# Block 0 of a hybrid encoder kernel: v and ca from unsplit fp32, low parts on the vector engine, and two changed load orders

## The chip, the cores and the metric

The kernel runs on one core of a Trainium2 chip. The core has a matmul engine (PE, with its weight loads shown as PEld), a vector engine (DVE), an engine for activation functions and copies (ACT), a general engine (POOL), a queue engine that issues most transfers (SP), and 16 DMA engines that all queues share. Each engine runs its own instructions in the order in which the compiler put them, and waits for the others by semaphores. The metric is the device time of one execution in microseconds, the median over several runs. "Granted clock" is the share of full speed at which the chip lets PE run.

## What is computed

One layer of an encoder trunk over 2048 tokens of width 1024, in float32. The parts that matter here:

```python
mod = silu(c) @ w_ada + b_ada                    # 1024 x 3072
shift, scale, gate = split(mod, 3)
h = rmsnorm(x, norm_g) * (1 + scale) + shift     # "adaLN"
u = h @ w_in + b_in                              # 1024 x 4364
mq, mk, mv, mo, mz, mi, mf, fq, fk, fv, fz, ff, ca, cg, cz = split(u)
ya = mlstm(silu(conv4(mq, mk)), mv, mi, mf, mo) * silu(mz)   # 4 heads of 128
yb = forgetting_attention(fq, fk, fv, ff) * silu(fz)         # 4 heads of 64, "fox"
yc = layernorm_silu(conv31(ca * sigmoid(cg))) * silu(cz)     # 256 channels
y = concat(ya, yb, yc) @ w_out
out = rmsnorm(x + gate * y, final_g)
```

## The kernel before, in words

**Blocks and units.** The tokens are worked in four blocks of 512 (b = 0 to 3). For each block `hprep` (L123) makes the normalised, modulated input h, transposed so that the 1024 features lie on the partitions as 8 tiles of 128 x 512. The columns of `w_in` are worked in units of 256 columns, in the order of the list `useq` (L200): v, ca, cg, then twice mv, mo, two of qk and mz, then fz, cz, f0 and f1. Units v, f0, f1 and fz are the attention's values, queries, keys and gate; ca, cg and cz are the convolution's; the m units are the mLSTM's. The last block has a slightly different order (v late). A unit with 128 weight columns as its left operand (`mm_cm`, L265) makes two groups of matmuls 128 x 512; one with tokens on its left (`mm_tm`, L277: v, mv, mo) makes four groups of 256 columns.

**Precision.** Products are made in the format fp32r, three for each pair of operands: the high part of a value is its copy in fp32r, the low part is what is left of it. So each of h and w is split in a high part (hh, wh) and a low part (hl, wl), and a group of 8 feature tiles has 24 matmuls: wh hh, wh hl and wl hh. A matmul of two plain fp32 operands exists too, in the mLSTM and in the sum for the gate, for example.

**Weights.** In block 0, `split_unit` (L161) loads each unit's two halves raw (512 KB each, tag "wr", two buffers), copies them to the high part on ACT (L177), subtracts on POOL for the low part (L178) and writes both parts to a scratch tensor `wd` in HBM from POOL's queue (L179, 1 MB for each half). In later blocks `reload_unit` (L184) loads the two parts back. The split tiles (tag "w") have four buffers, so two units. `prefetch` (L226) prepares the next unit; `load_unit` (L236) calls it when fewer than two are ready, then issues up to six pending steps of the 31-tap convolution on DVE (`backlog`, L433; 60 for each block), then a pending stage of the mLSTM, then a step of `wout_steps` (only in block 1: the output weights times the gate, split and stored).

**The start.** `ada_k` (L720) is called from `hprep(0)` between its steps. It loads the adaLN weights for shift and scale in four pieces of 2 MB (L714: two transfers of 1 MB each; three buffers, `WAB`), and, per piece, multiplies its eight 128 x 512 slices by silu(c): two on ACT (L737), six on DVE in two chains (L739), and adds the two (L741). Eight tiny matmuls (`pt_ada`, L746) sum over partitions, and three small DVE instructions make `shift` and `gs` for two feature tiles. Then ACT applies them to the transposed x (`hf`, L149), copies the high part (`hh`, L152), and POOL (six tiles) or DVE (two) subtracts (`hl`, L153). On SP's queue come in this order: the first adaLN piece, the four x tiles of 512 KB, raw v, the second piece, raw ca, the third and fourth pieces, small biases (`later`). The scaling of x by its norm is done by DVE (L139) in all blocks.

**The end.** After block 3's projections `prep_out` (L974) loads the split output weights, 1 MB for each of 8 feature tiles. The first (`EP` = 1) is issued ahead of f0's unit, two more ahead of f1's. The output projection's loads of y and x (`out_load`) are issued as it begins.

**Order.** The program lists its work in the order of the source; a scheduler orders each engine's instructions by a simulated timeline, with earlier ones first where both are ready. `tc.issue_after(i)` keeps what is issued in its block behind instruction i on the same engine. POOL cannot read PSUM, where matmuls land; DVE and ACT can.

Of the kernel before, what the change touches and what calls it, by code (L numbers as in the profile page):

```python
# [38 lines left out]
def tile_hybrid_trunk(  # L39
# [83 lines left out]
    def hprep(b, pre=None):  # L123
        xts = []
        if pre is not None:
            pre(-1)
        for tt in range(NTT):
            xt = xkpool.tile([P, D], F32, name=f"x{b}_{tt}", tag="x")
            with tc.issue_after(wload["mz0_1"]) if b == 1 else ExitStack():
                dma.dma_start(xt, x[0, b * TB + tt * P : b * TB + (tt + 1) * P, :])  # L130
            s2 = xpool.tile([P, 2], F32, name=f"s2{b}_{tt}", tag="s2", bufs=4)
            for n in range(2):
                sq = xpool.tile([P, TB], F32, name=f"sq{b}_{tt}{n}", tag="hf", bufs=HFB)
                s.activation(sq, xt[:, n * TB : (n + 1) * TB], AF.Square, accum_out=s2[:, n : n + 1])
# [3 lines left out]
            g.tensor_tensor(ss, ss, nhalf[:, 0:1], op=ALU.pow)  # L138
            v.tensor_scalar(xt, xt, ss, None, op0=ALU.mult)  # L139
            xts.append(xt)  # L140
        hi, lo = [], []
        for k in range(KT):
            if pre is not None:
                pre(k)
            pt = psx.tile([P, 512], F32, name=f"xT{b}_{k}", tag="x")
            for tt in range(NTT):
                pe.transpose(pt[:, tt * P : (tt + 1) * P], xts[tt][:, k * P : (k + 1) * P], ident)
            hf = xpool.tile([P, TB], F32, name=f"hf{b}_{k}", tag="hf", bufs=HFB)
            s.activation(hf, pt, AF.Identity, bias=shift[:, k : k + 1], scale=gs[:, k : k + 1])  # L149
            hh = hhpool.tile([P, TB], F32R, name=f"hh{b}_{k}", tag="hh")  # L150
            hl = hpool.tile([P, TB], F32R, name=f"hl{b}_{k}", tag="hl", bufs=HLB)
            s.copy(hh, hf)  # L152
            (g if b == 0 and k < HLV else v).tensor_tensor(hl, hf, hh.bitcast(F32), op=ALU.subtract)  # L153
            hi.append(hh)
            lo.append(hl)
        return hi, lo


    w_d, wload = {}, {}

    def split_unit(name, pieces, pool):  # L161

        width = sum(n for _, n in pieces)
        w_d[tuple(pieces)] = wd = scratch.tile([2, P, 8 * width], F32, name=f"wd_{name}")
        whs, wls = [], []
        for hf in range(2):
            wr = pool.tile([P, 4, 268], F32, name=f"wr_{name}_{hf}", tag="wr", bufs=2)[:, :, 0:width]
            o = 0
            for col, n in pieces:
                wload[name] = dma.dma_start(  # L170
                    wr[:, :, o : o + n],
                    dram(w_in, hf * 4 * P * DIN + col, [[DIN, P], [P * DIN, 4], [1, n]]),
                ).ins
                o += n
            flat, w4 = unit_tile(name, hf, width)
            wh, wl = w4[:, 0], w4[:, 1]
            s.copy(wh, wr)  # L177
            g.tensor_tensor(wl, wr, wh.bitcast(F32), op=ALU.subtract)  # L178
            g.dma_start(wd[hf], flat.bitcast(F32))  # L179
            whs.append(wh)  # L180
            wls.append(wl)
        return whs, wls

    def reload_unit(name, pieces):  # L184

        wd = w_d[tuple(pieces)]
        width = sum(n for _, n in pieces)
        whs, wls = [], []
        for hf in range(2):
            flat, w4 = unit_tile(name, hf, width)  # L190
            dma.dma_start(flat.bitcast(F32), wd[hf])
            whs.append(w4[:, 0])
            wls.append(w4[:, 1])
        return whs, wls
# [31 lines left out]
    def prefetch(pool=wraw):  # L226
        if upos[0] < len(useq):
            name, pieces = useq[upos[0]]
            uready.append((name, reload_unit(name, pieces) if tuple(pieces) in w_d else split_unit(name, pieces, pool)))
# [47 lines left out]
    def mm_tm(name, w, h, tt, width):  # L277
        ps = proj_psum(f"pt_{name}")
        cs = slice(tt * P, (tt + 1) * P)
        n = 0  # L280
        for k in range(KT):
# [125 lines left out]
    def units_conv(b, h):  # L407
        wa = load_unit(f"ca{b}")
        av = []
        for m in range(2):  # L410
# [5 lines left out]
            av.append(f)  # L416
        wg = load_unit(f"cg{b}")
# [266 lines left out]
    with tc.tile_pool(name="ada", bufs=4, side="right") as apool:  # L684
# [29 lines left out]
        def ada_load(jp):  # L714
            wt = apool.tile([P, KT, 2, 256], F32, name=f"wa{jp}", tag="wa", bufs=WAB)
            for i in range(2):
                dma.dma_start(wt[:, :, i, :], dram(w_ada, i * D + jp * 256, [[3 * D, P], [P * 3 * D, KT], [1, 256]]))
            wts.append(wt)

        def ada_k(j):  # L720
            if j < 0:
                ada_load(0)
                return
            if j == 0:
# [5 lines left out]
                for a in later:  # L730
                    dma.dma_start(*a)
            if j % 2:
                return
            wt = wts[j // 2]
            accs = [apool.tile([P, 2, 256], F32, name=f"wacc{j}{e}", tag=f"wacc{e}", bufs=1 + e) for e in range(2)]
            for k in range(2):
                s.activation(accs[k], wt[:, k], AF.Identity, scale=csil[:, k : k + 1])  # L737
            for k in range(2, KT):
                v.scalar_tensor_tensor(accs[k % 2], wt[:, k], csil[:, k : k + 1], accs[k % 2], op0=ALU.mult, op1=ALU.add)  # L739
# [10 lines left out]
            v.scalar_tensor_tensor(gs[:, j : j + 2], gs[:, j : j + 2], 1.0, cols[:, R_NG + j : R_NG + j + 2],  # L750
                                   op0=ALU.add, op1=ALU.mult)

        h = hprep(0, ada_k)

        pt = psx.tile([P, 512], F32, name="pt_cols2", tag="x")
        pe.transpose(pt[:, R_BQK:R_END], r3, ident[0 : R_END - R_BQK, 0 : R_END - R_BQK])
        pe.transpose(pt[:, 256:318], r2, ident[0:62, 0:62])
        v.tensor_copy(cols[:, R_BQK:R_END], pt[:, R_BQK:R_END])
        v.tensor_scalar(colsh, cols, 0.5, None, op0=ALU.mult)
        v.tensor_scalar(dww, pt[:, 256:318], 0.5, None, op0=ALU.mult)  # L760
        v.tensor_scalar(colse, cols[:, R_BFQ : R_BFQ + 2], 0.125, None, op0=ALU.mult)
# [257 lines left out]
    def outproj(qd):  # L1019
# [4 lines left out]
        if qd == 0:  # L1024
            for tt, n in ((0, 0), (0, 1), (1, 0)):
                if n == 0:
                    if tt:
                        out_load(qd, tt)
# [40 lines left out]
    for b in range(NB):  # L1069
        if b == 1:  # L1070
            side += wout_steps()
        if b < NB - 1:
# [64 lines left out]
    free_hh.append(1)  # L1137

# [37 lines left out]
EP = 1  # L1176
# [13 lines left out]
WAB = 3  # L1190
HLV = 6
# [29 lines left out]
```

## Time and profile before

| | us |
|---|---|
| median of 3 runs | 1361.3 |
| lowest, highest | 1360.88, 1370.79 |
| the profiled execution | 1369.51 |
| its span (first to last instruction) | 1367.7 |
| PE busy in the span | 1278.7 |
| DVE, ACT, POOL busy | 957.8, 561.9, 391.2 |
| mean granted clock | 0.979 |

The rows shown below are from the profiled execution. A group's row has: line, engine, operation, result and operands by the program's names, shape, count; then busy time in us and the mean of one in ns; then the idle time of the engine just before these instructions and which instruction ended it. A row of the timeline has start and length in us. A row of the list of waits has who waited for whom, us in total, times, the longest. In the table by stage each engine's busy us stand with the count of its instructions in brackets, then the granted clock, the DMA engines' busy share and the GB/s that they moved.

### The profile page before, as it was taken

The numbers are of one execution on the slowest core, as the hardware profiler recorded it, in microseconds if no ns is written. First come the engines' busy times: TensorE is split into PE (matmuls) and PEld (weight loads), VectorE is DVE, ScalarE is ACT, GpSimd is POOL, SyncE is SP. The second block draws the span as 40 slices with busy tenths as digits, with TensorE's granted clock in tenths as the row PEclk, the third lists the DMA queues.
The fourth block names the chain that finished last, engine by engine and source line by source line (L and its number), as shares of the span: only waits on it lengthen the run. The fifth ranks groups of instructions, "written<-read, shape, count | busy, mean of one in ns | idle before, by whom it ended". The sixth has DMA issues, their size and how long they took to land.

```text
span 1367.7 us, 21153 instructions
## 1 busy us (share of the span) xinstructions
PE 1278.7 (93%) x7399; PEld 1110.5 (81%) x7399; DVE 957.8 (70%) x2435; ACT 561.9 (41%) x1200; POOL 391.2 (29%) x445
## 2 busy tenths in 40 slices
PE   3799787999999999999999999998989999999997
PEld 2687576888989888989888889987777888888886
DVE  5579857865997764795653696675588687877742
ACT  4334415342243426231315232214466665756541
POOL 4365845520281120070110070120132221221221
PEclk9899889999999999999999999999999999999999
DMA  9784667779559968465557765459885665654231
GB/s 333 252 280 176 216 207 263 255 260 395 204 205 334 380 247 295 179 231 181 190 185 242 253 215 185 170 205 302 280 248 165 185 183 170 185 176 129 89 105 61
DMA packets 139945, 301.52 MB, mean 220 GB/s; under 512 B 13280, under 2 KB 80144, under 8 KB 121408
## 3 DMA queue, kind: packets, MB, share of 16 engines
q1 hardware_dynamic: 134528, 263.35, 57.6%
q0 software_dynamic: 5312, 36.83, 6.6%
q8 instruction: 58, 0.95, 0.3%
q14 instruction: 47, 0.39, 0.1%
HBM read 224.44 MB, written 75.69 MB: 219 GB/s over the span
## 4 chain that ended last, share of the span: by engine, by line
PE 77%; DMA 9%; DVE 8%; issue 2%; POOL 2%; ACT 1%; SPq 0%; POOLq 0%; DVEq 0%; ACTq 0%
PE po L1016 13%; PE pc_qk L272 10%; PE pc_f L272 7%; PE pt_mv L284 5%; PE pt_mo L284 5%; PE pc_mz L272 5%; PE ptr L882 4%; PE pc_fz L272 3%; PE pc_cz L272 3%; PE pc_ca L272 3%; DVE ac L433 2%; PE pa L870 2%; PE pt_v L284 2%; PE pa L869 2%; PE pc_cg L272 2%
## 5 line engine op out<-in xcount | busy, mean ns | idle before, releaser
L433 DVE SCALAR_TENSOR_TENSOR ac<-ca,dww,ac 128x512 f32<-128x512 f32 x240 | 186.6, 803 | 4.4 <-ACT ac L430 3.8
L1016 PE MATMUL po<-wo,yh 128*128 128x512 f32 x512 | 165.4, 399 | 4.6 <-ACT yh L1007 4.6
L272 PE MATMUL pc_qk<-hh,w_qk 128*128 128x512 f32 x512 | 163.2, 395 | 0.0
L843 ACT ACTIVATE S<-S,mx 128x512 f32<-128x512 f32 (+3 forms) x160 | 103.8, 652 | 49.1 <-DVE mx L841 44.5
L1016 PEld LDWEIGHTS po<-wo,yh 128*128 128x128 f32 x512 | 94.6, 190 | 24.1 <-ACT yh L1007 5.1
L272 PEld LDWEIGHTS pc_qk<-hh,w_qk 128*128 128x128 f32 x512 | 96.0, 188 | 21.5
L891 DVE TENSOR_TENSOR tl<-ptr,th 128x512 fp32r<-128x512 f32 (+1 forms) x144 | 92.1, 654 | 27.1 <-ACT th L890 25.3
L284 PE MATMUL pt_mv<-w_mv,hh 128*128 128x268 f32 (+1 forms) x512 | 98.0, 291 | 4.1 <-DMA w_mv<-wd_mv 3.1
L1016 PE MATMUL po<-wo,ya 128*128 128x512 f32 x256 | 100.9, 396 | 0.0
L272 PE MATMUL pc_qk<-hl,w_qk 128*128 128x512 f32 x256 | 100.5, 393 | 0.0
L833 POOL TENSOR_SCALAR_AFFINE_SELECT nd<-n 128x128 f32<-128x128 f32 (+1 forms) x64 | 30.3, 475 | 234.1 <-DVE mx L836 154.1
L890 ACT CAST th<-ptr 128x512 fp32r<-128x512 f32 (+1 forms) x144 | 76.6, 562 | 48.3 <-PE ptr L882 47.0
L284 PE MATMUL pt_mo<-w_mo,hh 128*128 128x256 f32 x512 | 93.4, 284 | 2.8 <-DVE G L291 1.5
L272 PE MATMUL pc_mz<-hh,w_mz 128*128 128x512 f32 x256 | 86.2, 411 | 8.6 <-POOL w_mz L178 8.6
L516 POOL COPY halo_m<-um 128x3 f32<-128x3 f32 x32 | 79.8, 2499 | 47.4 <-ACT um L515 47.4
L284 PEld LDWEIGHTS pt_mv<-w_mv,hh 128*128 128x128 f32 x512 | 82.1, 194 | 5.3 <-DMA w_mv<-wd_mv 3.3
L882 PE MATMUL ptr<-ident,S 128*128 128x128 f32 x544 | 83.4, 274 | 2.3 <-DVE mx L836 2.1
L272 PE MATMUL pc_f<-hh,w_f 128*128 128x512 f32 x256 | 84.8, 404 | 0.5 <-DVE vf L304 0.5
L284 PEld LDWEIGHTS pt_mo<-w_mo,hh 128*128 128x128 f32 x512 | 78.9, 189 | 3.5 <-issue 1.6
L522 DVE SCALAR_TENSOR_TENSOR am<-um,cols,am 128x512 f32<-128x512 f32 x96 | 73.5, 770 | 3.5 <-ACT am L519 3.2
L284 PE MATMUL pt_mv<-w_mv,hl 128*128 128x268 f32 (+1 forms) x256 | 74.5, 292 | 0.0
L284 PE MATMUL pt_mo<-w_mo,hl 128*128 128x256 f32 x256 | 72.6, 284 | 0.0
(273 smaller groups left out, 3262.4 us busy)
## 6 DMA issues: line engine op xcount, KB each, us to landing
w_qk<-wd_qk SPq DMA_DIRECT2D x24, 1024.0 KB, 7.3
w_mo<-wd_mo SPq DMA_DIRECT2D x12, 1024.0 KB, 10.2
w_mz<-wd_mz SPq DMA_DIRECT2D x12, 1024.0 KB, 5.1
w_f<-wd_f SPq DMA_DIRECT2D x12, 1024.0 KB, 4.7
n<-nb_d SPq DMA_DIRECT2D x36, 256.0 KB, 5.5
wa<-in_w_ada_dram SPq DMA_DIRECT2D x8, 1024.0 KB, 9.5
x<-in_x_dram SPq DMA_DIRECT2D x16, 512.0 KB, 8.8
wd_qk<-w_qk POOLq DMA_DIRECT2D x8, 1024.0 KB, 7.1
```

Source lines behind the costliest of these rows:

```text
L272: pe.matmul(ps, a, r, start=(n == 0), stop=(n == 3 * KT - 1))
L284: pe.matmul(ps[:, 0:width], a[:, cs], r, start=(n == 0), stop=(n == 3 * KT - 1))
L433: backlog.append(lambda acc=acc, u=u, i=2 * j + m, j=j: v.scalar_tensor_tensor(acc, u[:, j : j + TB], dww[:, i : i + 1], acc, op0=ALU.mult ...
L516: g.tensor_copy(halo_m[:, i, :], u[:, TB : TB + 3])
L522: v.scalar_tensor_tensor(acc, u[:, j : j + TB], cols[:, r + 8 * j : r + 8 * j + 1], acc, op0=ALU.mult, op1=ALU.add)
L833: g.affine_select(out=nb[:, 0:Wq], in_=L["n", ch][:, 0:Wq], pattern=[[-1, Wq]], compare_op=ALU.is_ge, fill=NEG, base=t0 - ch * TB, channel ...
L843: s.activation(Sb[:, 0:Wq], Sb[:, 0:Wq], AF.Exp, bias=mx[:, 4:5], accum_out=mx[:, 8 + ch : 9 + ch])
L869: pe.matmul(pa[:, 0:256], w, th[:, i, :], start=(kk == 0), stop=False)
L882: pe.transpose(pt[:, i, qi * P : (qi + 1) * P], Ps[qi][0][kk // TB][:, kk % TB : kk % TB + P], ident)
L890: s.copy(f(th), f(pt))
L891: v.tensor_tensor(f(tl), f(pt), f(th.bitcast(F32)), op=ALU.subtract)
L1016: pe.matmul(po, y[:, k], w[k][:, ns], start=(k == 0 and i == 0), stop=(k == 5 and i == 2))
```

## The change

1. In block 0 the units v and ca get no split: `raw_unit` loads plain fp32 weights, and `mm_cm` and `mm_tm` make 8 plain fp32 matmuls for each group, from `hf` (kept for all 8 tiles in `hf0`). The split of h (`h_split`) stands behind these two units in the source. v and ca are split in block 1 instead, and stored then.
2. The low parts of weights are subtracted by DVE. `split_unit` puts the subtraction and the store (still on POOL's queue) in a list `lows`, which `load_unit` works off behind the six convolution steps. h's low parts are all subtracted by DVE. For the units cg and mv0_0 the copy is ordered behind the last `hf`, the subtraction behind the last `gs`.
3. The four x tiles are loaded ahead of adaLN. An adaLN piece is two halves of 1 MB (four feature tiles each, two transfers of 512 KB), with four buffers for halves. All eight products run on DVE in one chain. cg's raw weights and the biases are issued behind adaLN. In blocks 1 to 3 ACT scales x, in block 0 DVE as before.
4. `prep_out(0)`, `(1)` and `(2)` are issued behind the reloads of v, f0 and f1 of block 3, and the first two `out_load` right behind the projections.

```diff
 def hprep(b, pre=None):
         xts = []
-        if pre is not None:
-            pre(-1)
...
-            v.tensor_scalar(xt, xt, ss, None, op0=ALU.mult)
+            if b:
+                s.activation(xt, xt, AF.Identity, scale=ss)
+            else:
+                v.tensor_scalar(xt, xt, ss, None, op0=ALU.mult)
             xts.append(xt)
+        if pre is not None:
+            pre(-1)
...
+            wload["hf"] = s.activation(hf, pt, AF.Identity, bias=shift[:, k : k + 1], scale=gs[:, k : k + 1]).ins
+            full.append(hf)
+            if b:
+                h_split(b, k, hf, hi, lo)
+        if not b:
+            pre(KT)
+            unit_v(b, (hi, lo, full))
+            conv_a.append(unit_ca(b, (hi, lo, full)))
+            for k in range(KT):
+                h_split(b, k, full[k], hi, lo)
         return hi, lo
+    def h_split(b, k, hf, hi, lo):
+        hh = hhpool.tile([P, TB], F32R, name=f"hh{b}_{k}", tag="hh")
+        hl = hpool.tile([P, TB], F32R, name=f"hl{b}_{k}", tag="hl", bufs=HLB)
+        s.copy(hh, hf)
+        v.tensor_tensor(hl, hf, hh.bitcast(F32), op=ALU.subtract)
+        hi.append(hh)
+        lo.append(hl)
 # split_unit
-            s.copy(wh, wr)
-            g.tensor_tensor(wl, wr, wh.bitcast(F32), op=ALU.subtract)
-            g.dma_start(wd[hf], flat.bitcast(F32))
+            first = name in ("cg0", "mv0_0")
+            with tc.issue_after(wload["hf"]) if first else ExitStack():
+                s.copy(wh, wr)
+
+            def low(wl=wl, wr=wr, wh=wh, flat=flat, hf=hf, first=first):
+                with tc.issue_after(wload["gs"]) if first else ExitStack():
+                    v.tensor_tensor(wl, wr, wh.bitcast(F32), op=ALU.subtract)
+                g.dma_start(wd[hf], flat.bitcast(F32))
+
+            lows.append(low)
+    def raw_unit(name, pieces, pool):
+
+        (col, width), = pieces
+        wrs = []
+        for hf in range(2):
+            wr = pool.tile([P, 4, 268], F32, name=f"wr_{name}_{hf}", tag="wr", bufs=4)[:, :, 0:width]
+            dma.dma_start(wr, dram(w_in, hf * 4 * P * DIN + col, [[DIN, P], [P * DIN, 4], [1, width]]))
+            wrs.append(wr)
+        return (wrs,)
 # load_unit
         for _ in range(min(TP, len(backlog))):
             backlog.pop(0)()
+        while lows:
+            lows.pop(0)()
 # mm_cm (mm_tm likewise)
+        if len(w) == 1:
+            for k in range(KT):
+                pe.matmul(ps, w[0][k // 4][:, k % 4, cs], h[2][k], start=(k == 0), stop=(k == KT - 1))
+            return ps
 # ada_load, ada_k
+            halves = []
+            for e in range(2):
+                wt = apool.tile([P, 4, 2, 256], F32, name=f"wa{jp}{e}", tag="wa", bufs=WAB)
...
+                prefetch(apool)
                 ada_load(1)
-                prefetch(wraw)
+                prefetch(apool)
                 ada_load(2)
                 ada_load(3)
...
-            for k in range(2):
-                s.activation(accs[k], wt[:, k], AF.Identity, scale=csil[:, k : k + 1])
-            for k in range(2, KT):
-                v.scalar_tensor_tensor(accs[k % 2], wt[:, k], csil[:, k : k + 1], accs[k % 2], op0=ALU.mult, op1=ALU.add)
-            acc = accs[1]
-            v.tensor_tensor(acc, acc, accs[0], op=ALU.add)
+            for k in range(KT):
+                wk = wts[j // 2][k // 4][:, k % 4]
+                if k == 0:
+                    v.tensor_scalar(acc, wk, csil[:, 0:1], None, op0=ALU.mult)
+                else:
+                    v.scalar_tensor_tensor(acc, wk, csil[:, k : k + 1], acc, op0=ALU.mult, op1=ALU.add)
 # end of the projections
-    for k in range(EP):
-        prep_out(k)
     unit_fqk(b, h, 0)
-    for k in range(EP, 7 - WSB):
-        prep_out(k)
     unit_fqk(b, h, 1)
+    for k, unit in enumerate(("v", "f0", "f1", "f1")[: 7 - WSB]):
+        with tc.issue_after(wload[f"{unit}{b}"]):
+            prep_out(k)
     left1.close()
...
+    for tt in range(2):
+        out_load(0, tt)
-WAB = 3
-HLV = 6
+WAB = 4
```

More of the change, by code (lines that the diff above doesn't have):

```diff
@@ L146, in hprep @@
             for tt in range(NTT):
[L147 to L155, printed above, removed]
-        return hi, lo
-    w_d, wload = {}, {}
+                wload["xT"] = pe.transpose(pt[:, tt * P : (tt + 1) * P], xts[tt][:, k * P : (k + 1) * P], ident).ins
+            if b:
+                hf = xpool.tile([P, TB], F32, name=f"hf{b}_{k}", tag="hf", bufs=HFB)
+            else:
+                hf = hf0[0].tile([P, TB], F32, name=f"hf{b}_{k}", bufs=1)
+            wload["hf"] = s.activation(hf, pt, AF.Identity, bias=shift[:, k : k + 1], scale=gs[:, k : k + 1]).ins
+            full.append(hf)
+            if b:
+                h_split(b, k, hf, hi, lo)
[5 more added lines that the diff above has]
+                h_split(b, k, full[k], hi, lo)
+        return hi, lo
+    def h_split(b, k, hf, hi, lo):
[5 more added lines that the diff above has]
+        lo.append(hl)
+    w_d, wload, lows, conv_a, hf0 = {}, {}, [], [], []
     def split_unit(name, pieces, pool):
@@ L224, in tile_hybrid_trunk, with prefetch @@
     side = []
-    def prefetch(pool=wraw):
+    def prefetch(pool=None):
         if upos[0] < len(useq):
             name, pieces = useq[upos[0]]
-            uready.append((name, reload_unit(name, pieces) if tuple(pieces) in w_d else split_unit(name, pieces, pool)))
+            if pool is not None:
+                w = raw_unit(name, pieces, pool)
+            elif tuple(pieces) in w_d:
+                w = reload_unit(name, pieces)
+            else:
+                w = split_unit(name, pieces, wraw)
+            uready.append((name, w))
             upos[0] += 1
@@ L280, in mm_tm @@
         n = 0
+        if len(w) == 1:
+            for k in range(KT):
+                pe.matmul(ps[:, 0:width], h[2][k][:, cs], w[0][k // 4][:, k % 4, 0:width], start=(k == 0), stop=(k == KT - 1))
+            return ps
         for k in range(KT):
@@ L714, in ada_load @@
         def ada_load(jp):
[L715 to L718, printed above, removed]
+            halves = []
+            for e in range(2):
+                wt = apool.tile([P, 4, 2, 256], F32, name=f"wa{jp}{e}", tag="wa", bufs=WAB)
+                for i in range(2):
+                    wload["ada"] = dma.dma_start(wt[:, :, i, :], dram(w_ada, (4 * e * P * 3 + i) * D + jp * 256,
+                                                       [[3 * D, P], [P * 3 * D, 4], [1, 256]])).ins
+                halves.append(wt)
+            wts.append(halves)
         def ada_k(j):
@@ L722, in ada_k @@
                 ada_load(0)
[L723 to L724 removed]
                 prefetch(apool)
                 ada_load(1)
[L727 removed]
+                prefetch(apool)
                 ada_load(2)
                 ada_load(3)
[L730 to L732 removed]
+                with tc.issue_after(wload["ada"]):
+                    for a in later:
+                        dma.dma_start(*a)
                 return
[L734 to L741 removed]
+            if j == KT:
+                pt = psx.tile([P, 512], F32, name="pt_cols2", tag="x")
+                with tc.issue_after(wload["xT"]):
+                    pe.transpose(pt[:, R_BQK:R_END], r3, ident[0 : R_END - R_BQK, 0 : R_END - R_BQK])
+                    pe.transpose(pt[:, 256:318], r2, ident[0:62, 0:62])
+                v.tensor_copy(cols[:, R_BQK:R_END], pt[:, R_BQK:R_END])
+                v.tensor_scalar(colsh, cols, 0.5, None, op0=ALU.mult)
+                v.tensor_scalar(dww, pt[:, 256:318], 0.5, None, op0=ALU.mult)
+                v.tensor_scalar(colse, cols[:, R_BFQ : R_BFQ + 2], 0.125, None, op0=ALU.mult)
+            if j % 2 or j == KT:
+                return
+            acc = apool.tile([P, 2, 256], F32, name=f"wacc{j}", tag="wacc", bufs=2)
+            for k in range(KT):
+                wk = wts[j // 2][k // 4][:, k % 4]
+                if k == 0:
+                    v.tensor_scalar(acc, wk, csil[:, 0:1], None, op0=ALU.mult)
+                else:
+                    v.scalar_tensor_tensor(acc, wk, csil[:, k : k + 1], acc, op0=ALU.mult, op1=ALU.add)
             pta = psx.tile([P, 512], F32, name=f"pt_ada{j}", tag="x")
@@ L749, in ada_k @@
             v.tensor_tensor(gs[:, j : j + 2], pta[:, 2:4], cols[:, r + 8 : r + 10], op=ALU.add)
-            v.scalar_tensor_tensor(gs[:, j : j + 2], gs[:, j : j + 2], 1.0, cols[:, R_NG + j : R_NG + j + 2],
-                                   op0=ALU.add, op1=ALU.mult)
+            wload["gs"] = v.scalar_tensor_tensor(gs[:, j : j + 2], gs[:, j : j + 2], 1.0, cols[:, R_NG + j : R_NG + j + 2],
+                                                 op0=ALU.add, op1=ALU.mult).ins
+        hf0.append(apool)
         h = hprep(0, ada_k)
[L755 to L761, printed above, removed]
     mpool = right.enter_context(tc.tile_pool(name="mpool", bufs=2, side="right"))
@@ L1175 @@
 BH = 2
-EP = 1
 PB = (3, 2, 3)
```

22 lines of the change are left out of this document (12 added, 10 removed).

## The prediction

> **What bounds the kernel now.** I read the profile's page first (busy time by engine, then the span in 40 slices):
>
> ```profile
> PE 1278.7 (93%) x7399; PEld 1110.5 (81%) x7399; DVE 957.8 (70%) x2435; ACT 561.9 (41%) x1200; POOL 391.2 (29%) x445
> PE   3799787999999999999999999998989999999997
> POOL 4365845520281120070110070120132221221221
> ```
>
> TensorE (PE) is the bound: 89 us of the span are not PE work, and the slices put them mostly in the first seven (34 us each) and little anywhere later. POOL is busy in just those slices. So the view to ask next is the busy time of each engine by stage. The stages are cut at the first matmul of the mLSTM value unit (mv): block 0's mv starts at 85.03, block 1's at 340.16, block 2's at 558.27 us, and from one to the next the same units run.
>
> ```profile
> core 0: us, PE busy (x) PEld busy (x) DVE busy (x) ACT busy (x) POOL busy (x), PEclk, DMA share, GB/s
> 2.50:20.00 17.50, 4.12 (x15) 2.83 (x15) 8.92 (x24) 8.76 (x21) 3.80 (x5) 1.00 1.03 351
> 23.00:52.00 29.00, 19.07 (x102) 16.30 (x102) 19.74 (x20) 10.62 (x16) 13.95 (x11) 0.88 1.05 374
> 20.00:73.83 53.83, 36.78 (x198) 31.95 (x198) 33.70 (x47) 19.19 (x32) 27.51 (x30) 0.87 0.77 262
> 85.03:340.16 255.13, 225.18 (x1274) 194.97 (x1272) 190.52 (x384) 95.22 (x161) 118.73 (x94) 0.95 0.72 257
> 340.16:558.27 218.11, 216.72 (x1277) 189.56 (x1276) 164.32 (x409) 83.27 (x159) 54.76 (x42) 1.00 0.76 275
> ```
>
> Two losses are seen. In the front the transfers are full (share 1.03 and 1.05) while PE has 36.78 us of work in 53.83. Then the first period takes 255.1 us where the second takes 218.1: 30 us of PE idle against 1.4, and a granted clock of 0.95 against 1.00. The list of waits of that first period, the groups by line of both periods, and the timeline of DVE (VectorE) and POOL (GpSimd) say why:
>
> ```profile
> PE pc_mz L272 <- POOL w_mz L178: 8.6, 2, 6.4
> PE pk L561 <- DVE am L526: 7.7, 3, 6.6
> PE ph L623 <- DVE hv L615: 6.7, 1, 6.7
> POOL w_qk L178 <- ACT w_qk L177: 32.4, 6, 10.6
> L433 DVE SCALAR_TENSOR_TENSOR ac<-ca,dww,ac 128x512 f32<-128x512 f32 x60 | 58.0, 989 | 1.1 <-ACT ac L430 0.9
> L433 DVE SCALAR_TENSOR_TENSOR ac<-ca,dww,ac 128x512 f32<-128x512 f32 x63 | 44.9, 740 | 1.1 <-ACT ac L430 0.9
> L526 DVE SCALAR_TENSOR_TENSOR am<-tm,am 128x512 f32<-128x512 f32 x8 | 10.2, 1275 | 3.9 <-ACT tm L525 3.9
> L526 DVE SCALAR_TENSOR_TENSOR am<-tm,am 128x512 f32<-128x512 f32 x8 | 5.4, 678 | 0.0
> L522 DVE SCALAR_TENSOR_TENSOR am<-um,cols,am 128x512 f32<-128x512 f32 x24 | 20.2, 842 | 0.0
> L522 DVE SCALAR_TENSOR_TENSOR am<-um,cols,am 128x512 f32<-128x512 f32 x24 | 17.5, 735 | 0.0
> 87.60 5.87 DVE L433 SCALAR_TENSOR_TENSOR ac<-ca,dww,ac 128x512 f32<-128x512 f32 x2
> 90.52 2.40 POOL L178 TENSOR_TENSOR w_mo<-wr_mo,w_mo 128x1024 fp32r<-128x1024 f32 x1
> 129.37 13.63 POOL L178 TENSOR_TENSOR w_mz<-wr_mz,w_mz 128x1024 fp32r<-128x1024 f32 x1 [1.80 <-ACT w_mz L177]
> ```
>
> The same DVE instruction takes 989 ns in the first period and 740 in the second (the pairs of rows are first period, second period). At 87.60 two of them take 5.87 us while POOL subtracts weights; at 129.37 it is POOL that waits, 13.63 us for a subtraction that takes 2.40 elsewhere, and PE stands 8.6 us for its result. The two engines stop each other.
>
> **The change part by part: the front.** These rows carry it:
>
> ```profile
> 41.89 8.52 DMA wa<-in_w_ada_dram
> wd_v<-w_v POOLq DMA_DIRECT2D x2, 1024.0 KB, 8.1
> 10.92 2.74 DVE L739 SCALAR_TENSOR_TENSOR wacc<-wa,csil,wacc 128x512 f32<-128x512 f32 x4 [6.50 <-ACT wacc L737]
> 28.09 9.76 DVE L739 SCALAR_TENSOR_TENSOR wacc<-wa,csil,wacc 128x512 f32<-128x512 f32 x6 [3.75 <-ACT wacc L737]
> 38.72 1.02 PE pt_ada L746 x8
> 39.60 1.52 PE L147 MATMUL xT<-ident,x 128*128 128x128 f32 x8
> 395.65 1.05 PE L655 MATMUL pt_gate<-gacc,ones 128*128 128x512 f32 x2
> L655 PE MATMUL pt_gate<-gacc,ones x4: 592/592/622, 395.7 to 401.8; 128*128 128x512 f32 x4
> 73.99 5.62 PE pc_cg L272 x24
> 311.17 3.34 PE pt_v L284 x28
> ```
>
> Today the last adaLN piece lands at 41.89 + 8.52 = 50.4 us, because four 1 MB writes of split v and ca weights go in between and because a third buffer had to come free. The change takes those writes out. What must have landed is x (2.1 MB), adaLN shift and scale (8.4) and raw v and ca (2.1): 12.6 MB, at 351 to 374 GB/s 34 to 36 us after 2.5, so 36 to 38.5 us. Four buffers of 1 MB hold two column pairs. The DVE frees a half in four instructions of 0.69 us, well before the queue comes to the next, so I cost that wait at nothing; if DVE fell behind by a whole pair it would be 5 us a pair. The DVE takes over the first two products from ACT and drops one addition: 8 x 0.69 = 5.5 us a pair against 4.9, but without POOL beside it the stretch at 28.09 (9.76 us for six) falls to 4.1.
>
> PE then is the slower part. An unsplit fp32 product is two instructions; two of 512 columns last 1.05 us in all and one 0.592, so they start 0.46 us apart (0.92 a product). ca is 16 products, 14.7 us; v is 32 of half the width, 14.7 us. The three-part form costs 24 in 5.62 us twice, 11.2, for ca and 96 x 0.119 = 11.5 for v (28 in 3.34). The fp32 form is **6.7 us dearer** on PE, and lies on the path. PE's front is then 29.4 + 32 transposes at 0.19 (1.52 for 8) 6 + 4 x 1.02 of pt_ada = 39.5 us; for a cold clock I add 3 (today 0.13 of 36.8, that is 4.8). It can begin when 4.2 MB are in (14.5 us) and DVE (2.7), pt_ada (1) and the first hf are through: about 19. So cg starts near 61.5 instead of 73.8, **gain 12**. Ends: not before the last landing (38) + 2.7 + 1 + 2 + the last pair's quarter of the work (7.4) = 51; not gained at all, and 6.7 dearer, 80.5. I take 61.5, since work adds up there without a wait. The split of h (8 copies and 8 subtractions) leaves the path to v and ca and lies under them; cg's raw weights land behind adaLN by about 42 and have 19 us for copy and subtraction. The x transfers ahead cost the first adaLN pair 6 us, which is in the 14.5.
>
> **The first period.** 13 weight units' low parts and block 1's v and ca (30 halves) go from POOL to DVE:
>
> ```profile
> L669 DVE TENSOR_TENSOR wor<-wor,woh x8: 1203/1218/1226, 411.7 to 469.8; 128x1024 fp32r<-128x1024 f32 x8
> L665 DVE TENSOR_TENSOR wor<-wor,gate 128x1024 f32<-128x1024 f32 x8 | 10.3, 1295 | 0.1
> L139 DVE TENSOR_SCALAR x<-x,ss 128x1024 f32<-128x1024 f32 x8 | 6.0, 750 | 2.5 <-POOL ss L138 2.4
> ```
>
> One such subtraction of this shape takes DVE 1.22 us (L669): +36.6 us. What contention adds today is, from the three pairs of rows above, 60 x 0.249 + 4.8 + 2.7 = 22.4 us at least. So DVE has about 190.5 - 22.4 + 36.6 = 205 us of work: more than in the second period (164), where PE yet never waits for it, and under 218. There DVE does two extra instructions of this size at each unit too (L665 and L669), with no stall of PE. The period's ends are 218 (as the second) and 255 or worse. With DVE at 94% of the lower end, I take the middle, 236: **gain 19**. The three waits quoted (23 us) are what would go; the next thing late is DVE itself. The low parts now stand in DVE's order behind six convolution steps, and wait there for ACT's copy; behind them wait evacuations. Block 1 gets raw v and ca instead of reloads of twice the bytes, with 4 copies and 4 subtractions; the f0 and f1 units (22 us of PE) cover it, and about 8 us would show if they did not. Moving 12 scalings of x (0.75 us each) to ACT is off the path: 0.
>
> **The end of the projections.** Three 1 MB output weights no longer go ahead of the fox weights, and two loads of y come earlier:
>
> ```profile
> 916.90 1.27 SPq L981 DMA_DIRECT2D wo<-wo_d  x3
> 920.61 1.26 SPq L191 DMA_DIRECT2D w_f<-wd_f  x2
> PE po L1016 <- ACT yh L1007: 4.6, 2, 2.9
> ```
>
> SP's queue is in order, so 2 MB of the 3 move behind w_f, which then lands some 5 us earlier; PE's idle there is small, and of the 4.6 us for yh one wait may go. Ends -4 to +6; **gain 2**, since they are first needed at 989 and either place is early enough.
>
> Sum: 12 + 19 + 2 = 33 us. The profiled execution ran 1369.5 us (span 1367.7), 8.2 above the median 1361.3; its 1336.5 corresponds to a median of **1328**.
>
> **The rivals.**
> DVE becomes the bound, by total or by order: the list above has POOL waiting 32.4 us for ACT's copies of w_qk, and some of that now holds DVE. The period stays at 250; gain 12 + 5 + 2, 1342 us. For: DVE is at 74% of this period already. Against: the second period.
>
> The front gains nothing, since PE stays cold or cg's split comes late: 19 + 2, 1340 us. For: 0.87 of clock today. Against: PE has denser work then.
>
> Slower: every unit's matmuls wait for a low part that stands in DVE's queue. POOL's w_mz cost PE 8.6 us for one unit. With w per unit over 13 units the period is 218 + 13w, and the 14 us of the rest are lost from w = 3.9. At w = 5: 283 us, +28 - 14, 1375 us. For: prefetch is one unit (11 us of PE) ahead. Against: 2.4 us of work, and the wout steps of the second period.
>
> POOL starves behind a denser DVE:
>
> ```profile
> L516 POOL COPY halo_m<-um 128x3 f32<-128x3 f32 x8 | 25.7, 3220 | 12.9 <-ACT um L515 12.9
> L514 POOL COPY um<-halo_m 128x3 f32<-128x3 f32 x8 | 8.9, 1119 | 7.4 <-DVE am L522 5.0 <-DVE dn L606 2.4
> ```
>
> In the second period these tiny copies take 3220 and 1119 ns. If PE waited for all 34.6 us, the period would be 253, gain 16, 1345 us. Against: PE idles 1.4 us there. The Trainium skill (SBUF — State Buffer, section Who interferes with whom) states this as a rule: an instruction of DVE with two SBUF inputs and one of GpSimd that reads SBUF exclude each other, and whichever comes second is blocked to the end of the first. By that rule the change moves the blocking to GpSimd's small copies rather than ending it; the trace agrees that both sides block (5.87 and 13.63 us), and gives the copies no weight for PE.
>
> Everything lands: the period is 218, gain 12 + 37 + 2, 1310 us.
>
> **How the numbers follow.** Forecast 0.55; DVE the bound 0.15; no gain in front 0.11; slower 0.07; POOL starves 0.04; everything 0.08. The range goes from 1304 to 1347: it takes in the gains of both ends but leaves half of "everything" and the slower case out. One per cent, 13.6 us, is about what a measurement of this kernel can tell from no change; faster means under 1347.7. Each case puts some weight past it: faster 0.82, same 0.11, slower 0.07.
>
> **What would show it.** Right: last adaLN piece at 36 to 39 us, cg's first matmul at 55 to 67, no 128x1024 subtraction on POOL, L433 near 740 ns in the first period, that period near 236 us, later periods as before. Wrong: PE waits for w_* from DVE in each unit, or cg later than 70.

## The result, and the profile after

| | before | after |
|---|---|---|
| median, us | 1365.68 (4 runs) | 1317.38 (4 runs) |
| lowest, highest | 1360.88, 1370.79 | 1313.24, 1322.12 |
| profiled execution (span) | 1369.51 (1367.7) | 1313.24 (1311.5) |

The ratio is 0.9647, with a 95% interval of 0.9585 to 0.9709: 48 us faster. The runs of either kernel lie in two groups some 8 us apart, and the profile of before was taken in its upper group, that of after in its lower one, so the two spans differ by 8 us more than the medians.

The page of the changed kernel, busy time and slices:

```profile
PE 1265.7 (97%) x7351; PEld 1095.5 (84%) x7351; DVE 939.7 (72%) x2467; ACT 567.3 (43%) x1204; POOL 301.8 (23%) x405
PE   4999999999999999999999999999889999999997
POOL 0116342102611200541010351121321122211221
```

PE is nearly full from the second slice on, and POOL's busy stretch at the start is much thinner (its first eight digits add up to 18, before to 40). The stages are cut where they were before: at the first matmul of cg, and at the first mv of each block (72.93, 291.70, 509.90 and 713.2 us in the changed kernel). From the timelines, in us:

| | cg starts | block 0's mv starts | first period | second | third | rest of the span |
|---|---|---|---|---|---|---|
| before | 73.8 | 85.0 | 255.1 | 218.1 | 203.0 | 606.4 |
| after | 61.45 | 72.9 | 218.8 | 218.2 | 203.3 | 598.3 |

The front gave 12 us, the first period 36, and the rest 8. The table by stage, the list of PE's waits in the first period (all four rows of it), and the groups by line there:

```profile
20.00:40.00 20.00, 18.70 (x70) 13.50 (x70) 15.50 (x29) 4.94 (x8) 0.00 (x0) 1.00 1.06 332
40.00:61.45 21.45, 20.57 (x94) 14.32 (x92) 12.28 (x31) 8.38 (x16) 1.83 (x3) 1.00 0.48 154
72.93:291.70 218.77, 216.13 (x1273) 188.93 (x1272) 179.50 (x411) 101.90 (x169) 60.92 (x72) 1.00 0.87 305
291.70:509.90 218.20, 216.82 (x1277) 189.61 (x1276) 160.82 (x402) 91.36 (x167) 47.54 (x42) 1.00 0.75 277
```

```profile
PE pt_mo L335 <- DVE so L557: 1.1, 1, 1.1
PE xT L150 <- ACT ac L523: 0.9, 1, 0.9
PE pt_v L335 <- DVE vf L355: 0.3, 1, 0.3
PE pn L655 <- DVE hv L663: 0.3, 1, 0.3
```

```profile
L488 DVE SCALAR_TENSOR_TENSOR ac<-ca,dww,ac 128x512 f32<-128x512 f32 x61 | 44.8, 762 | 2.0 <-ACT ac L485 1.9
L577 DVE SCALAR_TENSOR_TENSOR am<-um,cols,am 128x512 f32<-128x512 f32 x24 | 17.6, 737 | 0.0
L201 DVE TENSOR_TENSOR w_qk<-wr_qk,w_qk 128x1024 fp32r<-128x1024 f32 x8 | 9.7, 1218 | 1.3 <-ACT w_qk L197 1.3
L581 DVE SCALAR_TENSOR_TENSOR am<-tm,am 128x512 f32<-128x512 f32 x8 | 5.4, 673 | 0.2 <-ACT tm L580 0.2
L569 POOL COPY um<-halo_m 128x3 f32<-128x3 f32 x8 | 16.1, 2017 | 12.4 <-DVE am L577 12.4
L571 POOL COPY halo_m<-um 128x3 f32<-128x3 f32 x8 | 7.6, 948 | 2.4 <-ACT um L570 2.3
```

The first period is now as long as the second, PE idles 2.6 us in it, and its granted clock is 1.00 where it was 0.95. The convolution step is at 762 ns (989 before), the step `am<-tm` at 673 (1275). The low parts cost DVE 1.22 us each, yet DVE is busy for 179.50 us where it was for 190.52: it took on 36.6 us of work, gave 4 scalings of x (3 us) to ACT, and became 11 us less busy. So contention (an engine held up by the other) had cost it 190.5 + 36.6 - 3 - 179.5 = 45 us. This is the upper figure, since the busy time of a stage counts instructions that overlap only once; the groups that both kernels have there, added up one by one, are some 40 us shorter. Part of it sat in groups that the prediction didn't show, such as this one, first before and then after:

```profile
L573 DVE SCALAR_TENSOR_TENSOR ib<-am,ib 128x512 f32<-128x512 f32 x4 | 8.1, 2035 | 0.0
```

```profile
L628 DVE SCALAR_TENSOR_TENSOR ib<-am,ib 128x512 f32<-128x512 f32 x4 | 2.6, 681 | 0.0
```

### The profile page after: what moved, and what is told of

It is laid out like the page before. It is cut to its first block, busy times and chain, and to the rows that moved or that the text cites. A ratio compares the mean times of both kernels' runs of the same rounds, so it can differ in the third digit from the quotient of the medians.

```text
span 1311.5 us, 21066 instructions
## 1 busy us (share of the span) xinstructions
PE 1265.7 (97%) x7351; PEld 1095.5 (84%) x7351; DVE 939.7 (72%) x2467; ACT 567.3 (43%) x1204; POOL 301.8 (23%) x405
## 4 chain that ended last, share of the span: by engine, by line
PE 81%; DMA 8%; DVE 6%; ACT 1%; issue 1%; SPq 1%; POOL 0%; DVEq 0%; ACTq 0%; POOLq 0%
PE po L1076 13%; PE pc_qk L319 11%; PE pc_f L319 7%; PE pt_mo L335 5%; PE pt_mv L335 5%; PE pc_mz L319 5%; PE ptr L942 4%; PE pc_cz L319 3%; PE pc_fz L319 3%; PE pc_cg L319 3%; PE pc_ca L319 3%; PE pa L930 2%; PE pa L929 2%; PE pq L888 2%; PE pt_v L335 2%; PE pq L889 2%
## 5 line engine op out<-in xcount | busy, mean ns | idle before, releaser
L488 DVE SCALAR_TENSOR_TENSOR ac<-ca,dww,ac 128x512 f32<-128x512 f32 x240 | 174.1, 755 | 4.2 <-ACT ac L485 2.9
L571 POOL COPY halo_m<-um 128x3 f32<-128x3 f32 x32 | 76.3, 2389 | 43.9 <-ACT um L570 43.8
L319 PE MATMUL pc_mz<-hh,w_mz 128*128 128x512 f32 x256 | 83.1, 398 | 0.0
```

What stands on the lines that cost most here:

```text
L319: pe.matmul(ps, a, r, start=(n == 0), stop=(n == 3 * KT - 1))
L488: backlog.append(lambda acc=acc, u=u, i=2 * j + m, j=j: v.scalar_tensor_tensor(acc, u[:, j : j + TB], dww[:, i : i + 1], acc, op0=ALU.mult ...
L571: g.tensor_copy(halo_m[:, i, :], u[:, TB : TB + 3])
```

## The experiments

All times are medians; the ratio is to the kernel before, run beside it on the same chip. The changed kernel's own ratio is 0.9647 [0.9585, 0.9709].

**Low parts on POOL again.** One word of the changed kernel.

```diff
-                    v.tensor_tensor(wl, wr, wh.bitcast(F32), op=ALU.subtract)
+                    g.tensor_tensor(wl, wr, wh.bitcast(F32), op=ALU.subtract)
```

> The changed kernel with the weights' low parts subtracted by POOL again; all else as changed. Theory (the two engines block each other, so the subtraction costs DVE as much as it costs POOL): the first mv-to-mv period goes from 219 back to 245 to 255 us, the convolution steps from about 755 to 950 ns there, the time to 1340 to 1353. Rival (the period became short through the other parts: v and ca unsplit, fewer transfers, earlier start): the period stays under 227 us, the time under 1326.

Measured: 1362.8 us, ratio 1.000 [0.9974, 1.0025], more than the theory gave it (1340 to 1353). The whole gain is gone, although cg still starts early, at 62.6 us. Stage row, a group of DVE, one of POOL and a wait of PE in its first period:

```profile
74.09:337.68 263.59, 230.82 (x1273) 199.44 (x1272) 192.10 (x380) 103.13 (x170) 132.69 (x107) 0.92 0.72 256
```

```profile
L488 DVE SCALAR_TENSOR_TENSOR ac<-ca,dww,ac 128x512 f32<-128x512 f32 x60 | 60.4, 1029 | 1.1 <-ACT ac L485 0.9
L201 POOL TENSOR_TENSOR w_mz<-wr_mz,w_mz 128x1024 fp32r<-128x1024 f32 x4 | 21.0, 5252 | 4.3 <-ACT w_mz L197 4.3
PE pc_mz L319 <- POOL w_mz L201: 7.4, 2, 6.3
```

Convolution steps are back at 1029 ns, POOL's subtractions of w_mz take 5.25 us each, and PE waits for them. The first period is 8.5 us longer than before the change and the second 4.8 (222.9): the front's gain is given back. The units v and ca are now split in the first period too, which may be why it is longer; no run separates that. In the second period no weight is split; PE waits there once for DVE's `G`, 2.8 us.

**Low parts on DVE alone.** The same word, the other way, in the kernel before.

```diff
-            g.tensor_tensor(wl, wr, wh.bitcast(F32), op=ALU.subtract)
+            v.tensor_tensor(wl, wr, wh.bitcast(F32), op=ALU.subtract)
```

> The kernel before with that one part alone: the low parts of weights go from POOL to DVE, nothing else is changed. Theory: the first period falls from 255 to 220 to 232 us and the time by 23 to 35 us, to 1331 to 1343. Rival (it needs the other parts): less than 10 us.

Measured: 1333.06 us, ratio 0.9774 [0.9728, 0.982], 30 us faster, as the theory had it. The front is as slow as before (cg at 76.3):

```profile
87.54:308.42 220.88, 216.79 (x1273) 190.29 (x1272) 177.01 (x410) 94.85 (x161) 65.48 (x68) 0.99 0.84 300
```

One word moves the first period from 255.1 to 220.9 us, with all the rest of the kernel as before: 34 of the 36 us. Together the two runs say that the period's gain hangs on which engine subtracts.

**What in POOL's work does it: its reads, or that it is busy?** Two kernels put work on POOL that nobody uses, behind the store of each low part: two multiplications 128x512 (they read SBUF), or four memsets (they only write it). Both have one buffer of h's high parts less, to make room for the tile.

```diff
+    junk = const.tile([P, 512], F32, name="junk")
+    g.memset(junk, 0.0)
...
-                g.dma_start(wd[hf], flat.bitcast(F32))
+                st = g.dma_start(wd[hf], flat.bitcast(F32)).ins
+                with tc.issue_after(st):
+                    g.tensor_tensor(junk, junk, junk, op=ALU.mult)
+                    g.tensor_tensor(junk, junk, junk, op=ALU.mult)
...
-HHB = 14
+HHB = 13
```

> The changed kernel with two added POOL multiplications of 128x512 (both inputs in SBUF, result unused) behind every store of split weights, 34 times, about 2.4 us each time; to make room the buffers of hh go from 14 to 13. Nothing waits for them. Theory (blocking while POOL reads SBUF): convolution steps lengthen in the first period, which grows by 8 to 25 us. Rival 1 (only the delay until a low part was ready mattered, 2.4 against 1.2 us): no change, under 3 us. Rival 2 (POOL's small copies come late behind any long POOL work): as long as in the run with memsets.

> As the run with added multiplications, but with four POOL memsets of 128x512 in their place, about the same POOL time, which write SBUF and read nothing. Theory: convolution steps keep their 755 ns, the period grows by under 4 us. Rival 2: the period grows as in the run with multiplications.

Measured: 1353.21 us, ratio 0.9926 [0.9902, 0.995] with the multiplications; 1325.62 us, ratio 0.9738 [0.9662, 0.9815] with the memsets. First the kernel with reads, then the one with writes: stage row, the added instructions, the convolution step and PE's longest waits.

```profile
74.03:329.40 255.37, 227.97 (x1274) 196.95 (x1272) 219.57 (x411) 101.86 (x169) 147.05 (x134) 0.95 0.75 265
L207 POOL TENSOR_TENSOR junk<-junk 128x512 f32<-128x512 f32 x31 | 54.5, 1758 | 1.3
L206 POOL TENSOR_TENSOR junk<-junk 128x512 f32<-128x512 f32 x31 | 44.4, 1434 | 0.8
L493 DVE SCALAR_TENSOR_TENSOR ac<-ca,dww,ac 128x512 f32<-128x512 f32 x61 | 58.5, 986 | 2.0 <-ACT ac L490 1.9
PE pd L509 <- DVE ac L493: 7.1, 1, 7.1
PE pk L621 <- DVE am L586: 6.1, 1, 6.1
```

```profile
74.88:300.57 225.69, 218.19 (x1273) 190.79 (x1272) 181.45 (x410) 101.50 (x168) 123.50 (x196) 0.98 0.82 294
L206 POOL MEMSET junk<- 128x512 f32 x31 | 16.8, 542 | 0.2
L495 DVE SCALAR_TENSOR_TENSOR ac<-ca,dww,ac 128x512 f32<-128x512 f32 x60 | 44.5, 764 | 1.0 <-ACT ac L492 0.9
PE pt_mo L342 <- DVE so L564: 5.5, 1, 5.5
```

Both periods grew by more than the theory gave them (36.6 us for 8 to 25, and 6.9 for under 4). POOL is busy for much of either period (147 and 124 us), but only the reads slow DVE: 986 ns a convolution step against 764, DVE's busy time up by 40 us, and PE waits for DVE's results. The two added loads are alike where nothing holds them up: the shortest multiplication took 1.03 us, so 62 of them 64 us, and the memsets took 66. Nobody waits for POOL's added work itself, and what stands behind it on POOL comes late in both runs: DVE's longest wait for a value that POOL stores is 5.7 us with the multiplications and 7.0 with the memsets. So lateness isn't the cause of the 30 us between them. The Trainium skill (SBUF — State Buffer, section Who interferes with whom) says that a DVE instruction with two SBUF inputs contends with GpSimd instructions that read SBUF and not with those that only write it. These two runs agree: 255.4 against 225.7 us.

**The smaller buffer by itself,** since those two kernels shared it.

```diff
-HHB = 14
+HHB = 13
```

> The changed kernel with one buffer of h's high parts less (13 for 14), which the two kernels with added POOL work had too. Theory (the buffer was spare): cg near 61.5, the period within 2 us of 218.8, the kernel within 4 us of the changed kernel's 1317; then the 6.9 us that the period gained with the memsets comes from POOL being occupied. Rival (the buffer itself costs): the period near 225 and the kernel near 1324, then memsets cost nothing and the multiplications' whole price over them, some 30 us, is the blocking of DVE's and POOL's reads.

Measured: 1319.59 us, ratio 0.9678 [0.9647, 0.9709]; cg at 61.46, first period 219.2. The buffer was spare. The memsets' 6.9 us in the period are one wait of 5.5 us for DVE's `so`, in the last fence above, and a lower clock (0.98). The timeline of that kernel shows what held `so`:

```profile
149.14 0.52 POOL L416 DMA_DIRECT2D ir_d<-grib  x1
157.91 0.17 DVE L620 COPY dec<-ib 128x4 f32<-128x4 f32 x1 [6.95 <-DMA ib<-ir_d]
```

ACT had `grib` ready at 139.5 us, but POOL, among memsets and stores, issued its store at 149.14 (136.8 and 138.4 in the changed kernel). DVE stood idle for 6.95 us for the load of what was stored, and `so` stands behind that in DVE's order. So this smaller price is that of a busy POOL queue.

**How much can DVE take?** The prediction feared that DVE at 205 us would set the period. Three kernels add work to DVE behind each low part: it squares a quarter, three quarters or all of the raw weights in place. They are not read again.

```diff
                     v.tensor_tensor(wl, wr, wh.bitcast(F32), op=ALU.subtract)
+                v.tensor_tensor(wr[:, 0:3], wr[:, 0:3], wr[:, 0:3], op=ALU.mult)
```

> The changed kernel with a multiplication 128x768 on DVE behind each low part of a weight, which squares the raw weights in place (they are not read again), so that the output stays the same. 30 of them lie in the first period; at three quarters of 1.22 us each they add about 28 us to DVE, 179.5 + 28 = 207, about the 205 us that the prediction gave DVE. Theory (the prediction's step failed at DVE's load alone; its price for a load of 94% was right): the period goes from 218.8 to about 236, and the kernel to about 1335 us. Rival (the period would have reached its lower end at 205 us of DVE work too, and the middle between the ends was itself mis-chosen): the period stays under 224, the kernel under 1323. These multiplications have two SBUF operands, so POOL's small copies may wait longer.

> The same with the whole tile, 128x1024, 1.22 us each: 30 x 1.22 = 36.6 us more, DVE at 216 us of a period of 218.8. Theory (DVE's load sets the period from some 94% on): 240 to 260 us for the period, the kernel 1338 to 1360. Rival (DVE has enough slack in its order to be filled nearly wholly): the period at 219 to 230, the kernel under 1330.

> The changed kernel with a multiplication 128x256 on DVE behind each low part of a weight, on the raw weights in place (not read again; the output stays the same). 30 of them at 0.34 us add about 10 us: DVE at 190 us in the first period. With 179.5 us the period was 218.8, with 206.8 us 253.4. Theory (a load that is spread over the period has slack until DVE is near the length of the period, and the step lies between 190 and 207 us): the period at 219 to 223 and the kernel at 1315 to 1323 us. Rival (each microsecond on DVE shows in the period, since the convolution and the low parts stand in one order ahead of evacuations; on a straight line between the two points, 1.27 us for each): the period near 232 and the kernel near 1331.

Measured: 1321.99 us, ratio 0.9698 [0.9665, 0.9732] with a quarter; 1348.36 us, 0.9896 [0.9862, 0.9929] with three quarters; 1347.6 us, 0.9891 [0.9865, 0.9917] with all. The stage row of each, in this order, and for three quarters PE's longest waits:

```profile
72.72:299.47 226.75, 219.71 (x1273) 189.35 (x1272) 190.41 (x443) 103.21 (x170) 58.46 (x74) 1.00 0.84 298
```

```profile
74.94:328.31 253.37, 225.76 (x1273) 197.52 (x1272) 206.76 (x441) 103.59 (x170) 66.61 (x74) 0.93 0.76 272
L202 DVE TENSOR_TENSOR wr_qk<-wr_qk 128x768 f32<-128x768 f32 x8 | 7.6, 946 | 0.0
PE px L519 <- DVE ac L516: 8.4, 1, 8.4
PE ph L679 <- DVE hv L671: 6.2, 2, 5.1
PE pn L656 <- DVE dn L663: 5.5, 1, 5.5
```

```profile
74.40:325.19 250.79, 226.25 (x1274) 197.42 (x1272) 214.29 (x441) 103.60 (x169) 69.63 (x73) 0.93 0.75 269
```

| DVE busy in the first period, us | 179.5 | 190.4 | 206.8 | 214.3 |
|---|---|---|---|---|
| the period | 218.8 | 226.8 | 253.4 | 250.8 |

Neither side of the first expectation came out: at 207 us the period is neither 236 nor under 224, but 253. With all of the tile, at 214 us, it is in the theory's range. At 190 us it is 226.8, between the two numbers given, and the kernel's time lies in the theory's range (1315 to 1323). So DVE has no slack up to the length of the period. By one profile each, the first 11 us on DVE cost 8, the next 16 cost 27, and the last 8 nothing. The 8 us are more than the spread: the runs with the smaller buffer, the old order at the end and the first adaLN piece ahead, which leave this period as it is, have it at 217.5 to 219.2 us.

The three longest waits with three quarters lie close together, and this is the row of that stretch:

```profile
216.00:241.00 25.00, 4.91 (x21) 3.52 (x20) 19.66 (x75) 6.72 (x10) 6.74 (x9) 0.61 0.90 316
```

20 of PE's 27.6 us of idle time lie here, at a granted clock of 0.61. No convolution step is left on DVE then; `dn`, `ac` and `hv` stand there among the low parts of cz and f, the added multiplications and many small instructions of two norms. With all of the tile, 15 of 24.5 us lie in the same place (222 to 242 us). So it seems to count what stands in DVE's order ahead of the results that PE needs next, and not the sum alone; that may be why the last step is free.

The additions also do a second thing: they read the raw weights, so the two raw buffers come free later. ACT waits 61 us for raw weights with a quarter and 40 with three quarters, against 24 in the changed kernel. Of PE's own waits, those for weights are 2.6 of 6.8 us with a quarter, 2.3 of 27.6 with three quarters and 6.4 of 24.5 with all. The three runs therefore give no price for a microsecond of DVE work by itself.

**v and ca, split in block 0 as before.** Two kernels from the changed one: split and stored, and split but not stored (block 1 then splits them again, as the changed kernel does).

```diff
-            if b:
-                h_split(b, k, hf, hi, lo)
+            h_split(b, k, hf, hi, lo)
...
-                w = raw_unit(name, pieces, pool)
+                w = split_unit(name, pieces, pool)
```

> The changed kernel with v and ca in block 0 split again (three fp32r products, low parts on DVE, both parts stored to HBM in block 0, reloaded in block 1). Theory (PE's work sums up in the front, and unsplit saves 4.2 MB of stores while adaLN loads): PE saves 6.7 us of products, but the last adaLN half lands 5 to 11 us later; cg starts at 60 to 70 against 61.5 us, the time is 0 to 10 us above the changed kernel. Rival (the front gained through the unsplit form and nothing else): cg at 72 to 76, 11 to 15 us above.

> As the run before with v and ca split in block 0, but without storing the parts there; block 1 loads and splits them again, as in the changed kernel. Theory: adaLN lands as in the changed kernel, and PE has 6.7 us less to do while DVE and ACT have room; cg starts at 54 to 62 us, the time is between 7 us below and 2 us above the changed kernel. Rival (splits of h and w come late on the path to v and ca): cg later than 65, the time 4 us or more above.

Measured: 1326.48 us, ratio 0.9731 [0.9712, 0.975] with the store; 1319.44 us, 0.968 [0.9659, 0.97] without it. cg starts at 68.0 and 59.2. First the kernel that stores: DVE's last adaLN products and one of PE's waits for them in the timeline, and its front's row. Then the one that doesn't: its front's and first period's rows.

```profile
52.47 3.89 DVE L805 SCALAR_TENSOR_TENSOR wacc<-wa,csil,wacc 128x512 f32<-128x512 f32 x5
33.94 1.83 PE L810 MATMUL pt_ada<-one,wacc 128*128 128x1 f32 x8 [3.04 <-DVE wacc L805]
20.00:67.97 47.97, 39.26 (x211) 34.74 (x212) 30.67 (x58) 14.11 (x20) 5.70 (x18) 0.89 0.84 285
```

```profile
20.00:59.20 39.20, 34.97 (x211) 31.00 (x212) 30.96 (x60) 15.60 (x25) 2.68 (x7) 1.00 0.74 228
70.35:294.65 224.30, 218.82 (x1273) 191.88 (x1272) 181.51 (x411) 103.91 (x170) 62.01 (x73) 0.98 0.85 303
```

With the store, the last adaLN products end at 56.4 us (44.7 in the changed kernel), and cg is 6.5 us late: PE idles for 8.7 us from 20 us to there (2.2 in the changed kernel), at a granted clock of 0.89. Without the store the split form starts cg 2.3 us earlier than plain fp32 does in the changed kernel's profile: PE is busy for 35.0 us there against 39.3. The first period then takes 5.5 us longer, so nothing is left of it (why it does isn't settled). The plain fp32 form as such is worth nothing that these runs can tell; what pays is that 4 MB of writes are out of adaLN's way.

**The old order at the end.**

```diff
                 if n == 0:
+                    if tt:
+                        out_load(qd, tt)
...
     unit_v(b, h)
+    prep_out(0)
     unit_fqk(b, h, 0)
+    for k in range(1, 7 - WSB):
+        prep_out(k)
     unit_fqk(b, h, 1)
-    for k, unit in enumerate(("v", "f0", "f1", "f1")[: 7 - WSB]):
-        with tc.issue_after(wload[f"{unit}{b}"]):
-            prep_out(k)
...
-    for tt in range(2):
-        out_load(0, tt)
```

> The changed kernel with the order of the output weights and of the first two loads of y as before the change. Theory (most of the 8 us that the last stage fell by in the two profiles is variation between executions, since the kernel before with only the low parts moved shows 600.0 us there with the old order against 598.3): the last stage, from block 3's mv, is 598 to 603 us, the time 0 to 3 us above the changed kernel. Rival (the order gave the 8 us): 604 to 607 and 6 to 9 us above.

Measured: 1319.46 us, ratio 0.9666 [0.9641, 0.9691]. From block 3's mv to the end of the span it takes 599.6 us, the changed kernel 598.3. No gain of the new order can be told from zero, and the 8 us between the two profiles in that stretch are not its work.

**The first adaLN piece ahead of x.**

```diff
         xts = []
+        if pre is not None:
+            pre(-2)
...
         def ada_k(j):
+            if j == -2:
+                ada_load(0)
+                return
             if j < 0:
-                ada_load(0)
```

> The changed kernel with the first adaLN piece loaded ahead of x, the rest as changed. Theory (PE's front begins when both x and the first piece are in, whatever their order, and then work adds up): first hf and cg within 2 us of the changed kernel (hf at 22.9, cg at 61.5), the time within 3 us. Rival (x ahead was part of the front's 12 us): cg 3 to 6 us later.

Measured: 1312.54 us, ratio 0.9627 [0.9611, 0.9643]; cg at 61.6. The first fence has this kernel's first `pt_ada` and its last adaLN product on DVE, from the timelines, and the row of the stretch from PE's last wait to cg; the second has the changed kernel's:

```profile
14.13 1.86 PE L817 MATMUL pt_ada<-one,wacc 128*128 128x1 f32 x8 [10.68 <-DVE wacc L812]
43.20 0.75 DVE L812 SCALAR_TENSOR_TENSOR wacc<-wa,csil,wacc 128x512 f32<-128x512 f32 x1
44.16:61.57 17.41, 17.41 (x67) 11.83 (x67) 8.02 (x22) 7.54 (x15) 1.83 (x3) 0.90 0.59 181
```

```profile
19.49 1.87 PE L813 MATMUL pt_ada<-one,wacc 128*128 128x1 f32 x8 [16.05 <-DVE wacc L808]
44.00 0.74 DVE L808 SCALAR_TENSOR_TENSOR wacc<-wa,csil,wacc 128x512 f32<-128x512 f32 x1
45.73:61.45 15.72, 15.72 (x67) 10.94 (x67) 8.03 (x22) 7.55 (x15) 1.83 (x3) 1.00 0.52 168
```

PE starts 5.4 us earlier and cg no earlier: either way the adaLN chain on DVE ends near 44 us. PE's last wait is over 1.6 us earlier here, but the same 67 matmuls behind it take 17.4 us at a granted clock of 0.90, where they take 15.7 in the changed kernel at 1.00. The order of x is worth nothing that these runs can tell.

## Why the prediction was right, and where its sizes were off

**The mechanism** was right: DVE and POOL stopped each other in block 0's units, and the move ends it for DVE. No 128x1024 subtraction is left on POOL in the first period, the convolution step is near its later price, and the second and third periods are unchanged (218.2, 203.3). The sum was off: 33 us were forecast, to a median of 1328, and 48 came, to 1317.4. Most of the difference is one term, the first period.

**The front** was forecast to start cg at 61.5, and it starts at 61.45. The parts agree too: first `pt_ada` at 19.49 (forecast: PE begins at 19), and 41.96 us from there to cg (forecast: 39.5 + 3). The 3 us for a cold clock were not what filled it, since the granted clock is 1.00; from 20 us on PE was busy for 39.3 of 41.45 us, and 2.2 us were waits for ACT's `hf`. The agreement to a tenth is luck: in the profile of the run with the old order at the end, whose front is the same, cg starts at 63.4. The last adaLN transfer landed by 40 us: in the rows of the changed kernel below, the DMA share falls to 0.68 and then 0.06, while DVE no longer waits for data. Behind it on the queue come 0.64 MB of biases, 1.8 us at 350 GB/s, so an estimate is 38, within the forecast of 36 to 39.

```profile
36.00:38.00 2.00, 2.00 (x9) 1.69 (x10) 1.97 (x4) 1.52 (x3) 0.00 (x0) 1.00 1.11 350
38.00:40.00 2.00, 2.00 (x7) 1.09 (x6) 1.97 (x4) 0.00 (x0) 0.00 (x0) 1.00 0.68 186
40.00:42.00 2.00, 2.00 (x9) 1.38 (x8) 1.89 (x4) 0.00 (x0) 0.00 (x0) 1.00 0.06 13
```

The 6.7 us that plain fp32 was to cost PE showed as 4.3 us of busy time against the split form without a store, and as 2.3 us at cg's start, which is about the spread (61.45 and 63.4) of one front in two profiles.

**The first period** is the term that was mis-sized: forecast gain 19, measured 36. The 22.4 us that contention adds "at least" were put into the sum as its value. It is 40 to 45: the three groups that were quoted make up about half, and the rest sat in others (`ib<-am` took 2.04 us and takes 0.68 in the rows above). So DVE came to 179.5 us, not to 205, and the period to its lower end. The second half of that step, the middle between the ends for a DVE at 94%, was off the other way: at 206.8 us the period measured 253.4. The forecast of this term was too small by 17 because its load was wrong, not because DVE has room. Had contention been 22.4 us, 236 would have been some 17 us too short, judged by the run at 206.8 us, and that kernel's 1348.4 us lie above the upper end of the range, 1347. So two errors of opposite sign met here, and that the larger one went the good way is luck. The 8.6 us that PE waits for w_mz, which the prediction set beside one subtraction of 13.63 us, are two waits.

**The end of the projections** was given 2 us; the run with the old order finds no more than the spread between executions.

**The rivals.** POOL's small copies take longer in the first period than before the change (2.02 and 0.95 us each for three columns, 0.38 and 0.80 before; the shortest take 0.18). So part of the blocking did move to POOL's copies, as that rival had it, but PE's list of waits names none of the copies; the prediction gave them little weight, and that holds. No wait of PE for a low part is left in that list, so the slower case did not come. "DVE the bound" is wrong for this kernel; with 27 us more on DVE the period does go back to 253 us. "Everything lands" (12 + 37 + 2) was the nearest sum of all, with 12 + 36 + 0.

## What to carry to other kernels

When two engines stop each other, the time that the blocking costs is spread over all instructions of both; measure it as the difference of a whole stage's busy time, with the work that was added and taken away, and don't take the few groups that one looked at for the whole. One word that moves an operation in the old kernel, and the same word moved back in the new one, tells in two runs what of a large change does the work. An engine off the critical path that shares one queue between filler and results can set the time long before it is full: here the period grew by 8 us when added work, which also held the raw buffers longer, took DVE from 82% to 87% of 218.8 us. Look where the stalls lie before putting a price on the load: with three quarters of the tile added, 20 of 27.6 us lay in one stretch of 25.

## What was not expected of the hardware

POOL's reads cost time even where nobody needs POOL's result: two unused multiplications 128x512 per unit's half lengthened the period by 36.6 us, and the multiplications took 1.43 and 1.76 us in the mean, where the shortest took 1.03 and the longest 11.7.

In these runs a stall of PE cost more than its own length: with DVE at 206.8 us PE idled for 27.6 us of the period (2.6 in the changed kernel), and the same matmuls kept PE busy for 225.8 us instead of 216.1, at a granted clock of 0.93 instead of 1.00.
